# Row sums of squares taken from the transposed copy of x instead of a second load, with a new layout and order in the first phase of a decoder trunk

## The chip, the cores and the metric

The kernel runs on one core of a Trainium2 chip as one program. The metric is the device time of one execution in microseconds; three runs of the kernel before took 1880.76, 1881.30 and 1881.76. The profile comes from one further execution, taken by the hardware profiler.

The engines of a core work through their own queues and meet at semaphores: PE (TensorE) multiplies, ACT (ScalarE) evaluates functions and copies, DVE (VectorE) and POOL (GpSimd) do elementwise work, SP (SyncE) issues the DMA transfers. PEld is PE's loading of weights.

## The reference

The reference is one layer of a hybrid decoder: a mixer of two head groups, a cross-attention into memory tokens, and a gated FFN with a short convolution, for 1024 prompt tokens and 8 x 4 sample tokens (1056 rows of width 1024). The change lies in the beginning of the mixer:

```python
def rms_norm(x, g):
    xf = x.astype(jnp.float32)
    y = xf * lax.rsqrt(jnp.mean(xf * xf, axis=-1, keepdims=True) + EPS)
    return (y * g.astype(jnp.float32)).astype(x.dtype)
...
        u, v, cq, ckv, kpe = split_in(rms_norm(xp, g_mix[l]) @ w_in[l])
        a_out, _ = chunk_gmlp(u, v, w_s[l], b_s[l], ln_v_g[l], ln_v_b[l])
...
def chunk_gmlp(u, v, w_s, b_s, ln_g, ln_b):
    n, t, _ = u.shape
    c = min(t, CHUNK)
    vg = layer_norm(jax.nn.gelu(v).reshape(n, t // c, c, A_GROUPS, A_GROUP_DIM), ln_g, ln_b)
...
    out = jax.nn.gelu(u) * mixed.reshape(n, t, A_WIDTH)
```

## The kernel before

The tokens are numbered 0 to 1055 and cut in two ways: into nine tiles of 128 (`TILES`, the last of 32), and into three chunks of 384, 384 and 288 columns (`CH`). The function `phase1` (from L288) computes the mixer's projections of x. The scale of the norm is not multiplied into x: `rs_tok` (one number per token, tile i in column i) is the `scale` of the Gelu that reads each projection's result (L435 for v, L465 for u), so that products may run ahead of the sums of squares.

**x comes twice.** Transposed, features on the partitions, as `xT` (`xload`, L314 to L317; chunk c, half e of the eight feature blocks, tile `xr`), and once more by tokens, as `x` (`tload`, L319 to L322; 128 tokens of 4 KB each). The transposed copy is scaled by `g_mix` and split into a rounded part and its remainder: `xh` on ACT (L195) and `xl` on DVE (L198, which reads xr and xh). Weights are split in the same way (`wsplit`: `whi` on ACT L191, `wlo` on DVE L192). A projection of one tile (`proj`, L358) is then 24 matmuls: eight feature blocks times `whi·xh`, `wlo·xh`, `whi·xl` (L185). They accumulate in one of five PSUM buffers "mm", which come free when the Gelu of their tile has read them.

**The sums of squares** (`squares`, L324): for each token tile one Square on ACT with an accumulated sum (L332), then eleven small DVE steps for the reciprocal square root (`rsqrt`, L222 to L236). They come in four groups: tile 0; tiles 1 and 2; tiles 3 to 5; tiles 6 to 8.

**Order.** The SP queue is in written order (`manual_schedule`, L336): w_v0 half, chunk 0 half, twice; tile 0 of x; chunk 1; tiles 1 and 2; chunk 2; tiles 3 to 6 of x; w_u0, rows, w_s, w_v1, and tiles 7 and 8. On PE, ACT, DVE and POOL the order is a scheduler's, which places instructions by modelled times. The v projections of the nine tiles are followed by the small matmuls of `gate_matrices` (L394, L396) and the nine u projections; then the same with the second halves of v and u.

After Gelu, v goes in groups of tiles through a layer norm: mean (DVE L436), squares (ACT L440), square root, scaling (DVE L446), then gain and bias on POOL (L448, L450), then a split for the gate (`vgh`, ACT L191).

Of the kernel before, what the change touches and what calls it, by code (L numbers as in the profile page):

```python
# [13 lines left out]
P = 128  # L14
NP_, NS, NT = 1024, 32, 1056
# [5 lines left out]
TILES = [(i * P, P) for i in range(8)] + [(NP_, NS)]  # L21
# [64 lines left out]
def _layout(i):  # L86
# [5 lines left out]
    o["xT"] = f(x.T.reshape(8, P, NT).transpose(1, 0, 2))  # L92

    o["x"], o["mem"] = f(x), f(a["mem_prompt"][0])
    w_in = a["w_in"][0].reshape(8, P, 1568).transpose(1, 0, 2)

    def mtiles(w):
# [57 lines left out]
class Net:  # L155
# [132 lines left out]
    def phase1(self):  # L288
# [5 lines left out]
        pr = self.open("p1r", side="right")  # L294
        raws = {}

        def wraw(name, src, n):
            raws[name] = raw = self.t(pr, [P, 8, 288], F32, "wraw", 2)[:, :, :n]
            for k in range(0, 8, 4):
                nc.sync.dma_start(raw[:, k : k + 4], src[:, k : k + 4])  # L300

        def wsplit(name):
# [5 lines left out]
                self.split(hi[:, k : k + 4], lo[:, k : k + 4], raw[:, k : k + 4])  # L308
            return hi, lo

        px = self.open("px")
        xts, xrs = [], []

        def xload(c, e):  # L314
            o, n = CH[c]
            xrs.append(self.t(px, [P, 4, 384], F32, "xr", 6)[:, :, :n])
            nc.sync.dma_start(xrs[-1], I["xT"][:, 4 * e : 4 * e + 4, o : o + n])  # L317

        def tload(i, place):  # L319
            t0, tn = TILES[i]  # L320
            xts.append(place[:tn])
            nc.sync.dma_start(xts[-1], I["x"][t0 : t0 + tn])  # L322

        def squares(p, i0, i1):  # L324

            ss = self.t(p, [P, 4], F32, "ss", 2)[:, : i1 - i0]
            if i1 == 9:
                nc.vector.memset(ss, 1.0)
            for i in range(i0, i1):
                xt = xts[i]  # L330
                tn = xt.shape[0]
                nc.scalar.activation(xt, xt, AF.Square, accum_out=ss[:tn, i - i0 : i - i0 + 1])  # L332
            self.rsqrt(p, self.rs_tok[:, i0:i1], ss, 1.0 / 1024)

        xt = lambda: self.t(px, [P, 1024], F32, "xt", 3)
        loads = tc.manual_schedule(engines={mybir.EngineType.SP})  # L336
        loads.__enter__()
        raws["v0"] = raw = self.t(pr, [P, 8, 288], F32, "wraw", 2)[:, :, :256]
# [4 lines left out]
        tload(0, xt())  # L343
        for e in range(2):
            xload(1, e)
        tload(1, xt())
        tload(2, xt())
        for e in range(2):
            xload(2, e)
        w = wsplit("v0")  # L350
        for c, (o, n) in enumerate(CH):
            for k in range(8):
                self.split(xh[:, k, o : o + n], xl[:, k, o : o + n], xrs[2 * c + k // 4][:, k % 4], self.col("g_mix", k))
            if c == 0:
                squares(px, 0, 1)
            elif c == 1:
                squares(px, 1, 3)
        def proj(w, i, n):  # L358
            t0, tn = TILES[i]
            ps = self.t(pp, [P, 512], F32, "mm", 5)[:tn, :n]  # L360
# [5 lines left out]
        pl = self.open("pl")  # L366
        a_all = self.t(pl, [P, 9, 512], F32, "a_all")

        flat = a_all.rearrange("p i n -> p (i n)")
        for i in range(3, 7):  # L370
            tload(i, flat[:, (i - 3) * 1024 : (i - 2) * 1024])
        wraw("u0", I["w_u0"], 256)
        pg = self.open("pg")
        rows = self.t(pg, [P, 1024], F32, "rows")
        nc.sync.dma_start(rows, I["rows"][:, :1024].partition_broadcast(P))
        lng, lnb = rows[:, :512], rows[:, 512:]
        gates = {}

        def gate_matrices():

            ws = self.t(pg, [P, 8, P], F32, "ws")
            nc.sync.dma_start(ws, I["w_s"])
            nc.gpsimd.affine_select(ws, ws, [[0, 8], [1, P]], ALU.is_ge, 0.0, base=0, channel_multiplier=-1)
# [3 lines left out]
            sel = self.t(pg, [P, NS], F32, "sel")  # L387
            nc.sync.dma_start(sel, I["c_sel"])
            blk = self.t(pg, [NS, NS], F32, "blk")
            nc.sync.dma_start(blk, I["c_blk"])  # L390
# [3 lines left out]
            nc.tensor.matmul(st[:NS, :32], sel, wsc.rearrange("p g t -> p (g t)"), start=True, stop=True)  # L394
            o_bs, n_bs = COL["bsT"]
            nc.tensor.matmul(st[:NS, 32:40], sel, self.cols[:, o_bs : o_bs + n_bs], start=True, stop=True)  # L396
# [12 lines left out]
        wraw("v1", I["w_v1"], 256)  # L409
        nc.sync.dma_start(self.ident, I["c_ident"])  # L410
        for hf in range(2):
            c0 = hf * 256
            nu = 288 if hf else 256
# [5 lines left out]
            vgs = self.t(pg, [NS, 256], F32, "vgs")  # L419
            for i0, i1 in ((0, 3), (3, 6), (6, 8), (8, 9)):  # L420
                m, tn = i1 - i0, TILES[i0][1]
                if hf == 0 and i0 in (3, 6):
                    squares(pg, i0, i0 + 3)
                if hf == 0 and i0 == 3:
                    for i in range(7, 9):
                        tload(i, flat[:, (i - 7) * 1024 : (i - 6) * 1024])
                    wraw("u1", I["w_u1"], 288)
                    loads.__exit__(None, None, None)
                gv = self.t(pg, [P, 3, 4, 64], F32, "gv", 2)[:tn, :m]
                mu = self.t(pg, [P, 3, 4], F32, "mu", 2)[:tn, :m]  # L430
                rv = self.t(pg, [P, 3, 4], F32, "rv", 2)[:tn, :m]
                for i in range(i0, i1):
                    ps = proj(w, i, 256)
                    g, mi = gv[:, i - i0], mu[:, i - i0]
                    nc.scalar.activation(g.rearrange("p g d -> p (g d)"), ps, AF.Gelu_apprx_tanh, scale=self.rs_tok[:tn, i : i + 1])  # L435
# [19 lines left out]
                if hf == 0 and i0 == 0:  # L455
                    gate_matrices()
                    wsh, wsl, bs_s, wss = (gates[x] for x in ("wsh", "wsl", "bs_s", "wss"))
            if hf == 0:
                w = wsplit("v1")
                wraw("a0", I["w_a"][0], 256)  # L460
            else:
                w = wsplit("a0")
            for i, (t0, tn) in enumerate(TILES):
                ps = proj(wu, i, nu)
# [1084 lines left out]
    def out_proj(self, pp, p, mxs, ws, xh, xl, r3, end):  # L1549
# [4 lines left out]
        def chunk(m, c):  # L1554
            o, n = CH[c]
            wh, wl = ws[m]
            res = self.t(p, [P, 384], F32, "res", 4)[:, :n]
            nc.sync.dma_start(res, I["xT"][:, m, o : o + n])
# [726 lines left out]
```

## Time and profile before

| | value |
|---|---|
| runs, us | 1880.76, 1881.30, 1881.76 (median 1881.3) |
| the profiled execution, its own time, us | 1887.48 |
| its span, first to last instruction, us | 1885.8 |
| mean granted TensorE clock | 0.985 |
| busy PE / DVE / ACT / POOL, us | 1822.9 / 1380.2 / 927.5 / 715.1 |
| DMA over the span | 260.18 MB, mean 138 GB/s |
| DMA from 10 to 20 us | 387 GB/s |

A group row of the profile reads: line, engine, operation, tile written <- tiles read, partitions x elements, count | busy us, mean ns of one | idle time of the engine before them and what ended it. A row in time order begins with its start and its duration. Where several equal instructions follow one another they share a row, and x4 gives their number. Times inside the execution count from the first instruction.

### The profile page before, as it was taken

What the parts mean: (1) busy time and instruction counts of PE and PEld (TensorE: products, weight loads), DVE (VectorE), ACT (ScalarE), POOL (GpSimd) and SP (SyncE); (2) the same over time, 40 slices, a digit from 0 to 9 for tenths busy, and PEclk for the clock granted to TensorE, in tenths of its full rate; (3) what the DMA queues carried; (4) which work ended last, traced back from release to release, by engine and by line L of the source; (5) the groups of instructions that cost most, each with busy time, mean ns of one, the idle gap of its engine ahead of it and who ended that gap; (6) DMA issues with size and microseconds to landing.
All of it is one profiled execution on the core that took longest, in us unless ns stands there. A gap on an engine that the chain in (4) does not pass through costs nothing.

```text
span 1885.8 us, 39848 instructions
## 1 busy us (share of the span) xinstructions
PE 1822.9 (97%) x14402; PEld 1757.2 (93%) x14402; DVE 1380.2 (73%) x2883; ACT 927.5 (49%) x1965; POOL 715.1 (38%) x826
## 2 busy tenths in 40 slices
PE   6999899989999999999999999999999999999999
PEld 6999799889999999998799988999999999999999
DVE  6865967766777667776654676788888888879664
ACT  6435676666555555555443355633332333344442
POOL 1221515643544455444213100157677677500000
PEclk9999899999999999999999999999999999999999
DMA  8102204666765665664564335322222222395252
GB/s 294 60 10 69 80 1 163 228 223 186 213 196 167 187 179 169 175 170 148 171 177 134 134 134 163 128 80 69 91 69 94 77 69 80 99 363 164 79 153 76
DMA packets 135559, 260.18 MB, mean 138 GB/s; under 512 B 20417, under 2 KB 78626, under 8 KB 132290
## 3 DMA queue, kind: packets, MB, share of 16 engines
q1 hardware_dynamic: 134498, 256.58, 43.4%
q8 instruction: 114, 1.87, 0.4%
q10 hardware_dynamic: 864, 1.05, 0.2%
q14 instruction: 83, 0.68, 0.1%
HBM read 212.27 MB, written 45.30 MB: 137 GB/s over the span
## 4 chain that ended last, share of the span: by engine, by line
PE 60%; DVE 6%; issue 4%; DMA 3%; POOL 2%; SPq 1%; ACT 1%; POOLq 0%; DVEq 0%; ACTq 0%
PE d L185 12%; PE s L185 11%; PE b L185 7%; PE F L185 7%; PE X L185 6%; PE E L185 6%; PE A L185 3%; PE y L185 3%; DMA cT<-cT 1%; PE o L1348 1%; DVE mx L1299 1%; POOL S L1296 1%; PE t L185 1%; PE v L185 1%; SPq L1207 1%
## 5 line engine op out<-in xcount | busy, mean ns | idle before, releaser
L185 PE MATMUL s<-w2h,ch 128*128 128x288 f32 (+1 forms) x1024 | 303.8, 297 | 0.0
L185 PE MATMUL s<-w2h,cl 128*128 128x288 f32 (+1 forms) x1024 | 295.1, 288 | 2.7 <-POOL cl L1235 1.4
L185 PE MATMUL s<-w2l,ch 128*128 128x288 f32 (+1 forms) x1024 | 294.7, 288 | 0.0
L185 PEld LDWEIGHTS s<-w2h,ch 128*128 128x128 f32 x1024 | 192.6, 188 | 10.8 <-issue 8.3
L185 PEld LDWEIGHTS s<-w2h,cl 128*128 128x128 f32 x1024 | 192.4, 188 | 3.4 <-POOL cl L1235 1.9
L185 PEld LDWEIGHTS s<-w2l,ch 128*128 128x128 f32 x1024 | 192.8, 188 | 0.0
L1278 DVE TENSOR_REDUCE ss<-sq 128x16 f32<-128x1024 f32 x128 | 155.6, 1215 | 49.3 <-ACT sq L1275 48.4
L1235 POOL TENSOR_TENSOR cl<-cT,ch 128x512 fp32r<-128x512 f32 x64 | 83.7, 1307 | 160.7 <-ACT ch L1231 128.9
L1275 ACT ACTIVATE sq<-s 128x512 f32<-128x512 f32 x128 | 76.5, 598 | 90.0 <-PE s L185 90.0
L1272 ACT ACTIVATE sq<-s 128x512 f32<-128x512 f32 x128 | 76.8, 600 | 78.0 <-PE s L185 78.0
L191 ACT CAST a<-brb 128x528 fp32r<-128x528 f32 x77 | 48.8, 634 | 111.0 <-PE d L185 107.1
L185 PE MATMUL mm<-whi,xh 128*128 128x256 f32 (+3 forms) x288 | 84.5, 294 | 14.4 <-ACT xh L195 9.8
L185 PE MATMUL d<-a,w 128*128 128x264 f32 x768 | 95.4, 284 | 1.0 <-DVE G L2064 1.0
L192 DVE TENSOR_TENSOR a<-brb,a 128x528 fp32r<-128x528 f32 x77 | 54.4, 707 | 57.2 <-ACT a L191 57.1
L185 PEld LDWEIGHTS d<-a,w 128*128 128x128 f32 x768 | 94.3, 188 | 1.1 <-issue 1.1
L185 PE MATMUL mm<-wlo,xh 128*128 128x256 f32 (+3 forms) x288 | 83.3, 292 | 0.0
L185 PE MATMUL mm<-whi,xl 128*128 128x256 f32 (+3 forms) x288 | 83.2, 293 | 0.0
L930 PEld LDWEIGHTS o<-v,pth 128*128 128x128 f32 x576 | 75.9, 197 | 7.3 <-ACT pth L920 5.2
L930 PE MATMUL o<-v,pth 128*128 128x64 f32 x576 | 76.2, 274 | 4.8 <-ACT pth L920 4.4
L1935 POOL TENSOR_TENSOR lo<-s,hi 128x1024 fp32r<-128x1024 f32 x20 | 63.0, 3148 | 45.7 <-ACT hi L1934 45.7
L1231 ACT CAST ch<-cT 128x512 fp32r<-128x512 f32 x128 | 73.5, 627 | 3.9 <-DMA cT<-cT 3.9
L1990 ACT COPY a<-A 128x264 f32<-128x264 f32 x43 | 16.1, 375 | 118.7 <-PE A L185 114.9
(714 smaller groups left out, 6472.2 us busy)
## 6 DMA issues: line engine op xcount, KB each, us to landing
cT<-cT SPq DMA_DIRECT2D x256, 160.0 KB, 2.5
ck<-ck SPq DMA_DIRECT2D x256, 144.0 KB, 3.4
raw<-w_up SPq DMA_DIRECT2D x44, 512.0 KB, 3.6
wsumd<-wsum SPq DMA_DIRECT2D x13, 1024.0 KB, 4.3
actd<-cv SPq DMA_DIRECT2D x44, 264.0 KB, 2.6
brb<-actd SPq DMA_DIRECT2D x44, 264.0 KB, 5.9
wsum<-w_down SPq DMA_DIRECT2D x11, 1024.0 KB, 5.2
raw<-wsumd SPq DMA_DIRECT2D x20, 512.0 KB, 3.8
```

The source lines that it names most:

```text
L185: self.nc.tensor.matmul(out, l, r, start=first and i == 0, stop=last and i == len(seq) - 1)
L191: {"act": nc.scalar.copy, "pool": nc.gpsimd.tensor_copy, "dve": nc.vector.tensor_copy}[eng](hi, src)
L192: low = lambda: nc.vector.tensor_tensor(lo, src, hi, ALU.subtract)
L930: nc.tensor.matmul(u["o"][:, e], th[:, z * P : z * P + P], s["v"][:, jj, h % 4], start=j == z == 0, stop=e == 1 and jj == 2 * G + 1)
L1207: nc.sync.dma_start(ck[j * 32 : j * 32 + 32], I["ck"][bass.ds(rv, 1)].rearrange("a t s f -> (a t) s f"))
L1231: nc.scalar.copy(d["h"][:, k], src[k])
L1235: (nc.vector if k else nc.gpsimd).tensor_tensor(d["l"][:, k], src[k], d["h"][:, k], ALU.subtract)
L1272: nc.scalar.activation(sq[:, 0], ps[:, :, n0 : n0 + 256], AF.Square)
L1275: nc.scalar.activation(sq[:, 1], pt.rearrange("p (e d) -> p e d", e=2), AF.Square)
L1278: yield lambda: nc.vector.tensor_reduce(s["ss"][:, g0 : g0 + 2].rearrange("p e (z h) -> p z e h", z=2), sq.rearrange("p z e (h d) -> p z e ...
L1296: e.tensor_tensor(x, x, ss[:, g0:g1].rearrange("p g h -> p (g h)").unsqueeze(2).broadcast_to([P, n, 4]), ALU.mult)
L1935: eng.tensor_tensor(lo, src, hi, ALU.subtract)
```

## The change

- **Sums of squares.** The input `x`, its nine loads and the Squares by token tile are gone. ACT squares whole halves of the raw transposed chunk (`xr`, four feature blocks x 384 or 288 columns) into free space of `a_all`; POOL adds the two halves, then folds four blocks to two and to one; a matmul with ones over the partitions (`tok_sums`, L270) gives the sums of three tiles in a column each of a PSUM tile `st0`; `rsqrt` runs on three columns at a time, three times.
- **Layout.** `xT` is laid out by chunk, so that one half of a chunk is one run of 6144 B (4608 B) per partition, where it was four of 1536 B (1152 B). The weight tiles `wraw` are packed as well. The later load of `res` reads the same rows from their new place.
- **Warm-up.** `busy` issues four fp32 matmuls on a constant tile and one each on the raw weight half and the raw x half, into `st0`, which is overwritten later.
- **Order.** The v projections of tiles 0 to 5 are issued before the first sums; tiles 5 and 6 use PSUM buffers of the group "st". Tiles 6 and 7 stand behind the Gelu of tiles 0 to 2 in the program, tile 8 and the u projections of tiles 0 and 1 behind that of tiles 3 to 5. `gate_matrices` stands behind all of v. The loads of w_v1, w_s and two small tables move forward in SP's queue.

```diff
-        def squares(p, i0, i1):
-
-            ss = self.t(p, [P, 4], F32, "ss", 2)[:, : i1 - i0]
-            if i1 == 9:
-                nc.vector.memset(ss, 1.0)
-            for i in range(i0, i1):
-                xt = xts[i]
-                tn = xt.shape[0]
-                nc.scalar.activation(xt, xt, AF.Square, accum_out=ss[:tn, i - i0 : i - i0 + 1])
-            self.rsqrt(p, self.rs_tok[:, i0:i1], ss, 1.0 / 1024)
...
+            xrs.append(self.t(px, [P, 4, 384], F32, "xr", 6).rearrange("p k n -> p (k n)")[:, : 4 * n].rearrange("p (k n) -> p k n", k=4))
+            o = 8 * o + 4 * e * n
+            nc.sync.dma_start(xrs[-1].rearrange("p k n -> p (k n)"), I["xT"][:, o : o + 4 * n])
+
+        st0 = self.t(pp, [P, 512], F32, "st", 3)
+        warm = self.t(px, [P, 512], F32, "warm")
+        nc.vector.memset(warm, 1.0)
+
+        def busy(x, n):
+
+            for _ in range(n):
+                nc.tensor.matmul(st0[:, : x.shape[1]], warm[:, :P], x, start=True, stop=True)
+
+        flat = a_all.rearrange("p i n -> p (i n)")
+        places = ((0, 1536), (3072, 1536), (384, 1536))
+
+        def squares(c):
+
+            n = CH[c][1]
+            sq = [flat[:, a : a + 4 * n].rearrange("p (k n) -> p k n", k=4) for a in places[c]]
+            for e in range(2):
+                nc.scalar.activation(sq[e], xrs[2 * c + e], AF.Square)
+            add = lambda a, b: nc.gpsimd.tensor_tensor(a, a, b, ALU.add)
+            a = sq[0]
+            add(a, sq[1])
+            add(a[:, :2], a[:, 2:])
+            add(a[:, 0], a[:, 1])
+            acc = flat[:, places[c][0] : places[c][0] + 384]
+            self.pad(acc, c)
+            return acc
+
+        def roots(c, acc):
+            self.tok_sums(st0, acc, c, self.ones)
+            t = slice(3 * c, 3 * c + 3)
+            self.rsqrt(pl, self.rs_tok[:, t], st0[:, t], 1.0 / 1024)
...
+        busy(warm, 4)
...
+            if e == 0:
+                busy(raw[:, :2].rearrange("p k n -> p (k n)"), 1)
+                busy(xrs[0][:, 0, :256], 1)
...
+            accs.append(squares(c))
...
+        ready = {i: proj(w, i, 256, ("mm", 5) if i < 5 else ("st", 3)) for i in range(6)}
+        roots(0, accs[0])
...
                 if hf == 0 and i0 == 3:
-                    for i in range(7, 9):
-                        tload(i, flat[:, (i - 7) * 1024 : (i - 6) * 1024])
+                    ready[6] = proj(w, 6, 256, ("st", 3))
+                    ready[7] = proj(w, 7, 256)
+                    roots(1, accs[1])
...
+                elif hf == 0 and i0 == 6:
+                    ready[8] = proj(w, 8, 256)
+                    for i in range(2):
+                        us[i] = proj(wu, i, 256)
+                    roots(2, accs[2])
```

Three places show how the instructions stand now. The first is POOL's queue at its start, before: after the memset of `ones` its first work is the gain and bias of v (`gv`, L448, L450).

```order
L258 MEMSET ones_61 128x128
L448 ISA
L448 TENSOR_TENSOR gv_232<-gv_232,rows_217 128x256 x3
L450 TENSOR_TENSOR gv_232<-gv_232,rows_217 128x256 x3
L383 AFFINE_SELECT ws_361<-ws_361 128x1024
L392 COPY wsc_372<-ws_361 128x32
```

POOL's queue at the same place now: nine adds of squares (L343) stand ahead of v's gain and bias (now L469, L471), with the affine select of the gate matrix (`ws`) ahead of the last.

```order
L258 MEMSET ones_61 128x128
L343 ISA
L343 TENSOR_TENSOR a_all_90<-a_all_90 128x1536
L343 TENSOR_TENSOR a_all_90<-a_all_90 128x768
L343 TENSOR_TENSOR a_all_90<-a_all_90 128x384
L343 TENSOR_TENSOR a_all_90<-a_all_90 128x1536
L343 TENSOR_TENSOR a_all_90<-a_all_90 128x768
L343 TENSOR_TENSOR a_all_90<-a_all_90 128x1152
L343 TENSOR_TENSOR a_all_90<-a_all_90 128x384
L343 TENSOR_TENSOR a_all_90<-a_all_90 128x576
L402 AFFINE_SELECT ws_202<-ws_202 128x1024
L343 TENSOR_TENSOR a_all_90<-a_all_90 128x288
```

The adds of chunks 1 and 2 are interleaved; v's gain and bias come only when all are through.

The second place is DVE's queue now, from chunk 1's remainders on (`xr_112` and `xr_114` are its halves, `xr_116` and `xr_118` those of chunk 2, `wlo_378` belongs to w_u0, `st_94` holds the sums of squares).

```order
L198 SCALAR_TENSOR_TENSOR xl_83<-xr_112,cols_58,xh_82 128x384 x4
L198 SCALAR_TENSOR_TENSOR xl_83<-xr_114,cols_58,xh_82 128x384 x4
L198 SCALAR_TENSOR_TENSOR xl_83<-xr_116,cols_58,xh_82 128x288 x4
L198 SCALAR_TENSOR_TENSOR xl_83<-xr_118,cols_58,xh_82 128x288 x4
L192 TENSOR_TENSOR wlo_378<-wraw_191,whi_377 128x4x256
L222 TENSOR_SCALAR rqx_40_362<-st_94 128x3
L192 TENSOR_TENSOR wlo_378<-wraw_191,whi_377 128x4x256
L223 TENSOR_SCALAR rqy_42_364<-rqx_40_362 128x3
L224 TENSOR_SCALAR rqy_42_364<-rqy_42_364 128x3
```

Where before the square roots of tiles 0 to 2 stood among these remainders, all sixteen now come first, then the split of w_u0, then the root of tiles 0 to 2.

The third is ACT's queue now, with the Squares (L342) among the roundings of x (L195); `whi_377` belongs to w_u0.

```order
L195 ACTIVATE xh_82<-xr_110,cols_58 128x384 x4
L342 ACTIVATE a_all_90<-xr_110 128x1536
L195 ACTIVATE xh_82<-xr_112,cols_58 128x384 x4
L342 ACTIVATE a_all_90<-xr_112 128x1536
L195 ACTIVATE xh_82<-xr_114,cols_58 128x384 x4
L195 ACTIVATE xh_82<-xr_116,cols_58 128x288 x4
L195 ACTIVATE xh_82<-xr_118,cols_58 128x288 x2
L342 ACTIVATE a_all_90<-xr_114 128x1536
L195 ACTIVATE xh_82<-xr_118,cols_58 128x288 x2
L191 CAST whi_377<-wraw_191 128x4x256 x2
L342 ACTIVATE a_all_90<-xr_116 128x1152
L342 ACTIVATE a_all_90<-xr_118 128x1152
```

The Square of chunk 1's second half stands ahead of the last two roundings of chunk 2, and it writes where the first POOL add reads, so it comes after that add. The Gelu of tiles 0 to 2 stand behind these rows.

More of the change, by code (lines that the diff above doesn't have):

```diff
@@ L91, in _layout @@
     o = {}
[L92 to L94 removed]
+    xT = x.T.reshape(8, P, NT).transpose(1, 0, 2)
+    o["xT"] = f(np.concatenate([xT[:, :, c : c + n].reshape(P, 8 * n) for c, n in CH], 1))
+    o["mem"] = f(a["mem_prompt"][0])
     w_in = a["w_in"][0].reshape(8, P, 1568).transpose(1, 0, 2)
@@ L295, in phase1, with wtile @@
         raws = {}
+        def wtile(n):
+            return self.t(pr, [P, 8, 288], F32, "wraw", 2).rearrange("p k n -> p (k n)")[:, : 8 * n].rearrange("p (k n) -> p k n", k=8)
         def wraw(name, src, n):
-            raws[name] = raw = self.t(pr, [P, 8, 288], F32, "wraw", 2)[:, :, :n]
+            raws[name] = raw = wtile(n)
             for k in range(0, 8, 4):
@@ L309, in wsplit @@
             return hi, lo
+        pl = self.open("pl")
+        a_all = self.t(pl, [P, 9, 512], F32, "a_all")
         px = self.open("px")
-        xts, xrs = [], []
+        xrs = []
         def xload(c, e):
             o, n = CH[c]
[L316 to L322, printed above, removed]
@@ L342, in phase1 @@
             xload(0, e)
[L343 to L349, printed above, removed]
+            if e == 0:
+                busy(raw[:, :2].rearrange("p k n -> p (k n)"), 1)
+                busy(xrs[0][:, 0, :256], 1)
+        for c in (1, 2):
+            for e in range(2):
+                xload(c, e)
         w = wsplit("v0")
+        accs = []
         for c, (o, n) in enumerate(CH):
@@ L365, in phase1 @@
         self.close("px")
[L366 to L371, printed above, removed]
         wraw("u0", I["w_u0"], 256)
+        wraw("v1", I["w_v1"], 256)
         pg = self.open("pg")
@@ L376, in phase1 @@
         lng, lnb = rows[:, :512], rows[:, 512:]
+        ws = self.t(pg, [P, 8, P], F32, "ws")
+        nc.sync.dma_start(ws, I["w_s"])
+        sel = self.t(pg, [P, NS], F32, "sel")
+        nc.sync.dma_start(sel, I["c_sel"])
+        blk = self.t(pg, [NS, NS], F32, "blk")
+        nc.sync.dma_start(blk, I["c_blk"])
         gates = {}
         def gate_matrices():
-            ws = self.t(pg, [P, 8, P], F32, "ws")
-            nc.sync.dma_start(ws, I["w_s"])
             nc.gpsimd.affine_select(ws, ws, [[0, 8], [1, P]], ALU.is_ge, 0.0, base=0, channel_multiplier=-1)
@@ L454, in phase1 @@
                         nc.sync.dma_start(O["o_vg"][:, c0 : c0 + 256], vgs)
-                if hf == 0 and i0 == 0:
-                    gate_matrices()
-                    wsh, wsl, bs_s, wss = (gates[x] for x in ("wsh", "wsl", "bs_s", "wss"))
             if hf == 0:
+                gate_matrices()
+                wsh, wsl, bs_s, wss = (gates[x] for x in ("wsh", "wsl", "bs_s", "wss"))
                 w = wsplit("v1")
```

25 lines of the change are left out of this document (7 added, 18 removed).

## The prediction

> **What bounds the kernel now.** I read the page first, then the busy times by stretch of phase 1, then the instructions of each engine in time order.
>
> ```profile
> span 1885.8 us, 39848 instructions
> PE 1822.9 (97%) x14402; PEld 1757.2 (93%) x14402; DVE 1380.2 (73%) x2883; ACT 927.5 (49%) x1965; POOL 715.1 (38%) x826
> ```
>
> PE is busy in 97% of the span, so only what moves PE counts. The stretches (columns: busy time and instructions of PE, PEld, DVE, ACT, POOL, then granted PE clock, DMA share, GB/s) show where PE loses time early:
>
> ```profile
> 9.80:15.20 5.40, 5.40 (x25) 5.40 (x26) 5.15 (x9) 4.96 (x9) 0.00 (x0) 1.00 1.06 382
> 15.20:35.20 20.00, 20.00 (x169) 19.80 (x167) 15.31 (x61) 15.93 (x35) 0.00 (x0) 1.00 0.71 256
> 35.20:39.83 4.63, 0.00 (x0) 0.00 (x1) 4.49 (x20) 3.76 (x6) 0.00 (x0) 0.91 1.06 373
> 39.83:45.80 5.97, 5.97 (x28) 4.97 (x29) 5.82 (x13) 2.46 (x6) 5.96 (x7) 0.50 1.08 359
> 46.00:170.00 124.00, 124.00 (x917) 120.98 (x916) 82.50 (x262) 50.62 (x109) 29.21 (x35) 1.00 0.14 43
> ...
> PE mm L185 <- ACT gv L435: 4.6, 1, 4.6
> ```
>
> PE starts slowly (5.40/25 = 0.216 us a matmul), multiplies without a break from 15.2 to 35.2 (20.00/169 = 0.118), stands still for 4.63 us, then runs 28 matmuls at clock 0.50 (5.97/28 = 0.213 each, 28 x 0.095 = 2.7 us lost). After 46 it is busy 124.00 of 124.00 us. So whatever shifts phase 1 is carried on to the end, and this can be measured at one place: the first matmul of u tile 2, the first piece of PE work that stands behind the same set of matmuls in both kernels. Before, it follows the gate's two small matmuls:
>
> ```profile
> 51.02 0.25 PE L394 MATMUL st<-wsc,sel 128*32 128x32 f32 x2
> 51.11 0.21 PE L396 MATMUL st<-cols,sel 128*32 128x8 f32 x2
> 51.24 0.38 PE L185 MATMUL mm<-whi,xl 128*128 128x256 f32 x1
> ```
>
> The place is 51.3. The 4.63 us stall waits for a PSUM buffer, and that for the Gelu of tile 3, whose scale comes from squares of x that land late (ACT in time order):
>
> ```profile
> 9.13 2.13 ACT L195 ACTIVATE xh<-xr,cols 128x384 fp32r<-128x384 f32 x4 [1.72 <-DMA xr<-xT]
> 11.17 1.03 ACT L191 CAST whi<-wraw 128x1024 fp32r<-128x1024 f32 x1
> 12.64 2.13 ACT L195 ACTIVATE xh<-xr,cols 128x384 fp32r<-128x384 f32 x4 [0.44 <-DMA xr<-xT]
> 14.68 1.04 ACT L332 ACTIVATE xt<-xt 128x1024 f32<-128x1024 f32 x1
> ...
> 30.85 1.06 ACT L332 ACTIVATE a_all<-a_all 128x1024 f32<-128x1024 f32 x1 [1.29 <-DMA a_all<-x]
> ...
> 39.30 0.84 ACT L435 ACTIVATE gv<-mm,rs_tok 128x256 f32<-128x256 f32 x2 [0.18 <-DVE rs_tok L236]
> ```
>
> The change removes that load and so attacks a real stall: 4.63 + 2.7 = 7.3 us stand there, and 25 x 0.098 = 2.4 more at the start.
>
> **What it puts in its place.** Six Squares of whole raw halves on ACT, then nine adds on POOL (1536, 768, 384 columns for chunks 0 and 1; 1152, 576, 288 for chunk 2), all between 17 and 42, when DVE makes the xl halves of the split. Until now POOL did nothing there:
>
> ```profile
> 39.84 2.51 POOL L448 TENSOR_TENSOR gv<-gv,rows 128x256 f32<-128x256 f32 x3 [38.82 <-ACT gv L435]
> ```
>
> So this overlap is new, and I looked for other places where POOL adds while DVE reads two tiles from SBUF, as xl does (xr and xh). First the DVE, then the POOL rows:
>
> ```profile
> 64.88 0.70 DVE L224 TENSOR_SCALAR rqy<-rqy 32x4 int32<-32x4 int32 x1
> ...
> 67.01 0.67 DVE L235 SCALAR_TENSOR_TENSOR rqh<-rqa 32x4 f32<-32x4 f32 x1
> 67.71 0.15 DVE L236 SCALAR_TENSOR_TENSOR rqy<-rqh,rqy 32x4 f32<-32x4 f32 x1
> ...
> 64.77 1.49 POOL L448 TENSOR_TENSOR gv<-gv,rows 128x256 f32<-128x256 f32 x2 [6.14 <-DVE gv L446]
> 66.22 1.44 POOL L450 TENSOR_TENSOR gv<-gv,rows 128x256 f32<-128x256 f32 x2
> ```
>
> The DVE operations from 64.88 to 67.01, four of four columns each, take 0.66 to 0.70, one for each POOL operation, and 0.15 as soon as POOL is through. Each waits out one POOL operation, and POOL takes its turn after each. The same at full size:
>
> ```profile
> 1309.54 1.16 DVE L1958 TENSOR_TENSOR l<-raw,h 128x512 fp32r<-128x512 f32 x1
> 1310.63 3.52 DVE L2032 TENSOR_TENSOR G<-G,row 128x1056 f32<-128x1056 f32 x1
> ...
> 1281.55 1.26 DVE L2069 TENSOR_TENSOR cv<-cv,G 128x1056 f32<-128x1056 f32 x1
> ...
> 1310.12 2.91 POOL L2053 TENSOR_TENSOR cv<-cv,row 128x1056 f32<-128x1056 f32 x1
> 1312.98 2.33 POOL L1952 TENSOR_TENSOR s<-raw,raw 128x512 f32<-128x512 f32 x1
> ...
> L2040 DVE SCALAR_TENSOR_TENSOR cv<-G,cols,cv x44: 726/764/1772, 1221.9 to 1641.2; 128x528 f32<-128x528 f32 x22, 128x496 f32<-128x496 f32 x22
> ```
>
> L2032 needs 1.26 alone (L2069, same shape) and took 3.52: it ended at 1314.15, 1.12 after POOL's L2053 at 1313.03. L1952 waited for it in turn. L2040, an operation of xl's own kind, shows the wait as well (median 0.764, longest 1.772). [...]
>
> **The sum, step by step.** Prices first (group rows: count, busy time and mean in ns; then rows of DVE in time order):
>
> ```profile
> L1337 POOL TENSOR_TENSOR S<-S,bc 128x1056 f32<-128x1056 f32 x7 | 17.3, 2474 | 7.6 <-ACT bc L1336 7.6
> L1296 POOL TENSOR_TENSOR S<-S,ss 128x768 f32<-128x768 f32 x8 | 16.1, 2013 | 47.5 <-DVE ss L236 47.5
> L1383 POOL TENSOR_TENSOR raw<-raw,cols 128x1024 f32<-128x1024 f32 x4 | 7.6, 1898 | 6.8 <-DVE xl L192 3.2 <-DMA raw<-w_mq 3.1 <-DMA res<-res 0.5
> L1935 POOL TENSOR_TENSOR lo<-s,hi 128x1024 fp32r<-128x1024 f32 x20 | 63.0, 3148 | 45.7 <-ACT hi L1934 45.7
> L383 POOL TENSOR_SCALAR_AFFINE_SELECT ws<-ws 128x1024 f32<-128x1024 f32 x1 | 1.3, 1287 | 0.0
> ...
> 12.23 1.23 DVE L192 TENSOR_TENSOR wlo<-wraw,whi 128x1024 fp32r<-128x1024 f32 x1 [0.25 <-ACT whi L191]
> 13.38 2.20 DVE L198 SCALAR_TENSOR_TENSOR xl<-xr,cols,xh 128x384 fp32r<-128x384 f32 x4
> 16.04 0.15 DVE L223 TENSOR_SCALAR rqy<-rqx 128x1 int32<-128x1 int32 x1
> 16.22 0.15 DVE L224 TENSOR_SCALAR rqy<-rqy 128x1 int32<-128x1 int32 x1
> ...
> L198 DVE SCALAR_TENSOR_TENSOR xl<-xr,cols,xh 128x288 fp32r<-128x288 f32 x8 | 3.9, 515 | 0.0
> ```
>
> 1. *When POOL begins.* A Square of 1536 columns is not in the trace; 1.04 for 1024 gives at most 1.56 and, with a fixed part, about 1.45. xh of the first half ends at 11.26; Square to 12.7; the cast to 13.7; the second xh (2.13, pitch about 2.05) to 15.75; Square to 17.2.
>
> 2. *Adds.* L1337 is 2.474/1056 = 2.34 ns a column: 3.6 for 1536, 2.7 for 1152, 1.35 for 576, 0.9 for 384 (I take 1.0), 0.7 for 288 (0.8); L1296 gives 2.0 for 768. Chunks 0 and 1: 6.6 each; chunk 2: 4.85; the scheduler puts the affine select (1.3) ahead of the last add. Sum 19.35. Bounds: by L1383 (1.85 ns) 18.05 x 1.85/2.34 + 1.3 = 15.6; by L1935 (3.07 ns, which has waits in it) 25.0.
>
> 3. *xl.* Behind 17.2 stand eight of 384 at 2.20/4 = 0.55 and eight of 288 at 0.515: 8.5. One that has waited is about 0.14 shorter (1.12 against 1.26, and L2053's 1313.03 - 1310.70 = 2.33 against 2.47); for 19 hand-overs that is -2.7.
>
> 4. *The last xl.* If the two take turns, nothing overlaps: 17.2 + 19.35 + 8.5 - 2.7 = 42.4. Where POOL waits for a Square (about 24.5 to 26.5) DVE runs several xl on end, which the sum has already. Without any waits ACT's last xh, near 27, would set it, the last xl near 27.7. The loss is 14.7 us on DVE. Part of it PE hides: tile 3 waits for chunk 1's first xl, and tile 6 takes its eight steps one by one as the xl of chunk 2 come, so it ends at 42.6 instead of about 30.4.
>
> 5. *rs_tok.* In DVE's queue behind the last xl stand two wlo of u (1.23 each, the first step of the square root between them) and ten more steps, 0.18 apart for one column and taken as 0.2 for three: 2.45 + 2.0 = 4.5, so 46.9. Gelu of tile 0 (0.84/2 = 0.42) ends at 47.3. Tile 7 needs its PSUM buffer: PE stalls from 42.6 to 47.4, 4.8 us, as long as the stall that was removed.
>
> 6. *PE from there to u tile 2*: tiles 7, 8, u0, u1, 96 matmuls. A stall of 4.63 was followed by 28 matmuls at 0.213, so I take that again: 6.0 + 68 x 0.118 = 14.0; the two sums by ones (18 small matmuls and their waits, an estimate from the gate's small ones above, 0.1 apiece less overlap) 1.1; gate 0.3. 47.4 + 15.4 = 62.8. The Gelu of tile 3, whose buffer u tile 2 takes, comes at about the same time, behind casts that wait for six POOL operations of 0.84 to 0.91 (2.51 and 2.73 for three, L448, L450).
>
> 62.8 - 51.3 = **+11.5 us**. The other parts: four constant and two raw multiplications on PE before 9 lie in its idle time, and where they raise PE's speed at the start (2.4 us above), tiles 0 to 2 still wait for xh and xl and end before the first held xl, so they gain nothing here. Longer runs: DMA ran at 387 GB/s between 10 and 20 already (x rows of 4 KB and xT rows of 1.5 KB mixed), 0; the loads of v1, ws, sel and blk land earlier than they are needed, 0. The 4.3 MB of x fall out of a DMA that no longer decides, 0.
>
> [...]
>
> The profiled execution took 1887.48 (span 1885.8 and 1.7 around it), the median of the three runs 1881.3. Profiled I expect 1887.5 + 11.5 = 1899.0, timed 1881.3 + 11.5 = **1892.8**.
>
> **Rivals.**
>
> *No waits between POOL and DVE (faster).* [...] For it: ACT and PE are left alone by POOL, and L198 itself has never been seen beside POOL. Against it: every row above. It decides if xl stays near 0.55 after 17.2.
>
> *POOL starves instead (no change).* If DVE's queue, which is full, keeps the memory until its xl are through, the adds begin near 27.7; chunk 0's end at 34.3, and Sq1b, which needs a buffer of the first add, comes at 31.3, with the last two xh behind it. [...] Against it: L1952 got its turn after one DVE operation, and so did each L448.
>
> *Longer adds and a lower clock during the dribble of tile 6 (slower still).* By L1935's price +5.65, 17.2 in all: 1898.5. Against it: its rows include waits. By L1383's price -3.75: +7.7, 1889.0; with the clock kept after the stall another -2.7, 1886.3.
>
> **Chances.** Turns, at any of these prices: 0.77. No waits: 0.14. POOL starves, or losses and gains balance: 0.09. Differences under 0.2% (3.8 us) can hardly be told from no change; the cases fall on its three sides: slower 0.77, same 0.09, faster 0.14. The likeliest case alone spans 1886.3 to 1898.5; the range, 1882 to 1900, also takes in gains that offset part of the wait, and leaves the faster case out.
>
> **What would show it.** Right: POOL's L343 of 1536 columns at 17.2, 3 to 4 us long; beside it an xl of about 3.5, then xl of 1.3 to 3 one after each add; the last xl between 38 and 47; PE idle for 4 to 5 us ahead of tile 7; u tile 2 near 63, and PE without gaps behind it. Wrong: xl at 0.5 to 0.6 throughout (the first rival), POOL waiting until 27 (the second), or a later phase with idle PE time in which the shift is lost; before 170 there is none, and behind it I have only the 97%.

## The result, and the profile after

| | before | changed |
|---|---|---|
| runs, us, median | 1881.73 (6 runs, 1880.76 to 1884.43) | 1893.87 (6 runs, 1893.13 to 1896.65) |
| ratio, 95% interval | | 1.0065, 1.0054 to 1.0076 |
| profiled execution / its span | 1887.48 / 1885.8 | 1894.05 / 1892.2 |
| u tile 2 begins in the profile | 51.6 | 60.4 |

The change is 12.1 us slower; 1892.8 was forecast. The prediction takes 51.3 for the start of u tile 2 before, from the row at 51.24. By count that row is the last matmul of u tile 1: it is number 264, the end of the eleventh projection of 24, and a `whi,xl`, the kind with which every projection ends. The first of u tile 2 stands behind it, here before and then changed:

```profile
51.56 0.38 PE L185 MATMUL mm<-whi,xh 128*128 128x256 f32 x1
...
60.44 0.39 PE L185 MATMUL mm<-whi,xh 128*128 128x256 f32 x1 [0.77 <-ACT gv L456]
```

Some of POOL's and DVE's rows in time order (start, duration) show the chunk sums beside the split of x. First POOL, then DVE, of the changed kernel:

```profile
15.99 3.49 POOL L343 TENSOR_TENSOR a_all<-a_all 128x1536 f32<-128x1536 f32 x1 [14.98 <-ACT a_all L342]
19.56 2.02 POOL L343 TENSOR_TENSOR a_all<-a_all 128x768 f32<-128x768 f32 x1
25.35 3.94 POOL L343 TENSOR_TENSOR a_all<-a_all 128x1536 f32<-128x1536 f32 x1 [2.49 <-ACT a_all L342]
31.28 2.86 POOL L343 TENSOR_TENSOR a_all<-a_all 128x1152 f32<-128x1152 f32 x1
...
16.45 3.45 DVE L198 SCALAR_TENSOR_TENSOR xl<-xr,cols,xh 128x384 fp32r<-128x384 f32 x1 [0.58 <-ACT xh L195]
19.82 2.17 DVE L198 SCALAR_TENSOR_TENSOR xl<-xr,cols,xh 128x384 fp32r<-128x384 f32 x1
23.20 0.61 DVE L198 SCALAR_TENSOR_TENSOR xl<-xr,cols,xh 128x384 fp32r<-128x384 f32 x1
31.55 2.90 DVE L198 SCALAR_TENSOR_TENSOR xl<-xr,cols,xh 128x288 fp32r<-128x288 f32 x1
38.41 1.05 DVE L198 SCALAR_TENSOR_TENSOR xl<-xr,cols,xh 128x288 fp32r<-128x288 f32 x1
```

The xl issued at 16.45 ends at 19.90, 0.42 behind POOL's end at 19.48: it waited for the add, or was held by it, as it is called below. POOL waits in its turn: the add of 1536 columns at 25.35, issued while an xl ran, took 3.94, the one at 15.99, when none ran, 3.49. The third DVE row falls where POOL waits for a Square, and is back at 0.61. The same from a distance, the group rows of the stretch from 15 to 41:

```profile
L198 DVE SCALAR_TENSOR_TENSOR xl<-xr,cols,xh 128x288 fp32r<-128x288 f32 x8 | 14.0, 1822 | 0.0
L198 DVE SCALAR_TENSOR_TENSOR xl<-xr,cols,xh 128x384 fp32r<-128x384 f32 x10 | 10.6, 1126 | 0.6 <-ACT xh L195 0.6
```

Chunk 2's xl takes 1822 ns where it took 515. The last of them ends at 39.88. PE's waits (us in total, times, longest) and stretches (columns as in the prediction):

```profile
PE mm L185 <- ACT gv L456: 4.7, 2, 4.0
PE mm L185 <- DVE xl L198: 3.0, 2, 1.6
PE st L185 <- DVE xl L198: 2.2, 3, 1.0
...
20.00:30.00 10.00, 8.53 (x46) 8.18 (x47) 10.00 (x9) 9.76 (x16) 7.36 (x4) 0.66 0.51 204
40.70:44.67 3.97, 0.03 (x1) 0.00 (x0) 3.06 (x13) 0.50 (x2) 0.00 (x0) 0.50 0.40 108
44.67:50.50 5.83, 5.81 (x35) 5.74 (x35) 5.40 (x21) 2.87 (x6) 0.00 (x0) 0.66 0.37 148
62.00:180.00 118.00, 118.00 (x868) 115.40 (x867) 79.53 (x255) 46.77 (x103) 29.62 (x34) 1.00 0.10 30
```

The stall of 4.63 at 35 is gone; one of 3.97 at 40.7, again followed by a half-speed stretch, and 5.2 us of waits for xl stand in its place. The clock was also down between 20 and 30 (0.66), which the prediction's sum does not have; it moves nothing here, since PE still waits 2.2 us for xl in tile 6 behind it. Behind 62 PE has no gap to 180.

### The profile page after: what moved, and what is told of

Its sections match the earlier page's. It is cut to its first block, busy times and chain, and to the rows that moved or that the text cites. A ratio compares the mean times of both kernels' runs of the same rounds, so it can differ in the third digit from the quotient of the medians.

```text
span 1892.2 us, 39881 instructions
## 1 busy us (share of the span) xinstructions
PE 1832.5 (97%) x14432; PEld 1762.9 (93%) x14432; DVE 1394.1 (74%) x2872; ACT 924.0 (49%) x1953; POOL 738.8 (39%) x836
## 3 DMA queue, kind: packets, MB, share of 16 engines
q1 hardware_dynamic: 127154, 252.25, 42.7%
## 4 chain that ended last, share of the span: by engine, by line
PE 61%; DVE 5%; issue 4%; DMA 3%; POOL 2%; SPq 2%; ACT 1%; POOLq 0%; DVEq 0%; ACTq 0%
PE d L185 12%; PE s L185 12%; PE b L185 7%; PE F L185 7%; PE X L185 7%; PE E L185 7%; PE A L185 3%; PE y L185 3%; PE o L1368 1%; DMA cT<-cT 1%; DVE mx L1319 1%; POOL S L1316 1%; DMA raw<-mix 1%; SPq L1223 1%; SPq L1227 1%
## 5 line engine op out<-in xcount | busy, mean ns | idle before, releaser
L185 PEld LDWEIGHTS s<-w2h,ch 128*128 128x128 f32 x1024 | 193.0, 189 | 10.8 <-issue 8.3
L185 PE MATMUL mm<-whi,xh 128*128 128x256 f32 (+3 forms) x272 | 79.7, 295 | 4.7 <-ACT gv L456 4.7
L185 PE MATMUL mm<-whi,xl 128*128 128x256 f32 (+3 forms) x272 | 78.8, 294 | 3.0 <-DVE xl L198 3.0
L185 PE MATMUL mm<-wlo,xh 128*128 128x256 f32 (+3 forms) x272 | 78.1, 290 | 0.0
```

What stands on the lines that cost most here:

```text
L185: self.nc.tensor.matmul(out, l, r, start=first and i == 0, stop=last and i == len(seq) - 1)
```

## The experiments

All of them in one table first. "At 100 us" is the median, over the PE, ACT and DVE instructions of 100 to 180 us that both traces have equally often, of their start less their start in the second profile of before (below); by this the first profile of before stands at +0.9. The time is less the median of the runs of before taken with it.

| kernel | u tile 2 | at 100 us | timed against before, us | ratio, 95% interval |
|---|---|---|---|---|
| the change | 60.4 | +9.8 | +12.1 | 1.0054 to 1.0076 |
| adds_dve | 53.2 | +4.1 | +4.1 | 1.0007 to 1.0039 |
| pool_writes | 50.8 | +2.9 | +4.8 | 1.0010 to 1.0030 |
| no_busy | 60.8 | +10.0 | +9.3 | 1.0036 to 1.0064 |
| old_layout | 61.1 | +10.8 | +11.3 | 1.0035 to 1.0063 |
| early_space | 45.4 | -2.0 | -0.2 | 0.9987 to 1.0017 |
| kept_load | 41.4 | -7.5 | -9.1 | 0.9935 to 0.9963 |
| kept_load_cold | 42.7 | -7.4 | -6.5 | 0.9958 to 0.9982 |
| mended | 52.2 | +1.8 | +3.6 | 1.0006 to 1.0031 |
| adds_twice | 77.1 | +40.7 | +41 (one run) | |

**adds_dve.** Is xl long because of POOL's adds (the turns of the prediction), or because the Squares come late?

```diff
-            add = lambda a, b: nc.gpsimd.tensor_tensor(a, a, b, ALU.add)
+            add = lambda a, b: nc.vector.tensor_tensor(a, a, b, ALU.add)
```

> The nine adds of the squares run on DVE instead of POOL; nothing else is edited (the scheduler then spreads them among the xl operations of chunks 1 and 2). Theory (a POOL add and an xl exclude each other, so POOL's 21 us of adds and gate work are added to DVE's time): the adds cost DVE about 1.04 ns a column, 7392 columns or 7.7 us instead, no xl is longer than 0.65, the last xl ends near 29 to 31 (changed kernel: 39.8), and u tile 2 starts at 48 to 50.5 instead of 60.4: about 10 us faster than the changed kernel, 1882 to 1885. Rival (the late sums come from ACT's Squares and the order, and xl is only long because it waits for something else): DVE's queue grows by 7.7 us while nothing leaves it, so u tile 2 comes later than 60.4 and the time is 1895 to 1902.

Measured: 1886.21 (11 runs), 7.7 less than the change. Some of DVE's rows:

```profile
17.50 1.76 DVE L343 TENSOR_TENSOR a_all<-a_all 128x1536 f32<-128x1536 f32 x1
19.18 1.67 DVE L198 SCALAR_TENSOR_TENSOR xl<-xr,cols,xh 128x384 fp32r<-128x384 f32 x3
25.61 1.75 DVE L343 TENSOR_TENSOR a_all<-a_all 128x1536 f32<-128x1536 f32 x1
27.28 3.07 DVE L198 SCALAR_TENSOR_TENSOR xl<-xr,cols,xh 128x288 fp32r<-128x288 f32 x5
31.14 0.50 DVE L198 SCALAR_TENSOR_TENSOR xl<-xr,cols,xh 128x288 fp32r<-128x288 f32 x1
```

More work on DVE ends its xl sooner, at 31.6 instead of 39.9: the rival falls. The one xl above 0.65 (1.35) is among the five at 27.28; it stands beside the affine select, which was left on POOL. The gain is smaller than expected (53.2, not 48 to 50.5): this execution's first xh came at 9.59, 1.6 later than the change's, and the scheduler put the small adds and two square roots between each other, so that rs_tok of tiles 0 to 2 is ready only at 38.8. Before tile 7 PE waits 4.2 us for sums.

**pool_writes.** Is it POOL's being busy, or its reading? The sums of squares become constants here, so rs_tok, and what hangs on it, is not computed.

```diff
-            add = lambda a, b: nc.gpsimd.tensor_tensor(a, a, b, ALU.add)
+            add = lambda a, b: [nc.gpsimd.memset(a, 0.125) for _ in range(3)]
```

> Each add on POOL is replaced by three memsets of the same target, so POOL is busy for about as long (0.9 ns a column and memset, 1.4 us three times for 1536) but reads nothing; the sums of squares are then constants, so that part of the result is left out. Theory (what excludes xl is POOL's reading of SBUF): xl stays at 0.5 to 0.65 beside a busy POOL, the last xl ends at 26 to 28, u tile 2 starts at 45 to 48, 1879 to 1883. Rival (any long POOL instruction holds DVE up, or the waits come from semaphores between POOL and the others, which all stay): xl of 1.5 to 4 us beside the memsets, last xl near 38 to 42, 1892 to 1896.

Measured: 1886.99 (12 runs). POOL's memsets, and some of DVE's rows beside them:

```profile
13.66 18.51 POOL L343 MEMSET a_all<- 128x1536 f32 x22
...
17.06 2.21 DVE L198 SCALAR_TENSOR_TENSOR xl<-xr,cols,xh 128x384 fp32r<-128x384 f32 x4 [0.59 <-ACT xh L195]
20.46 2.21 DVE L198 SCALAR_TENSOR_TENSOR xl<-xr,cols,xh 128x384 fp32r<-128x384 f32 x4 [1.19 <-ACT xh L195]
26.55 1.81 DVE L198 SCALAR_TENSOR_TENSOR xl<-xr,cols,xh 128x288 fp32r<-128x288 f32 x4 [0.96 <-ACT xh L195]
28.27 0.16 DVE L222 TENSOR_SCALAR rqx<-st 128x3 f32<-128x3 f32 x1
28.47 3.09 DVE L223 TENSOR_SCALAR rqy<-rqx 128x3 int32<-128x3 int32 x1
28.77 2.78 DVE L192 TENSOR_TENSOR wlo<-wraw,whi 128x1024 fp32r<-128x1024 f32 x1
31.59 0.60 DVE L224 TENSOR_SCALAR rqy<-rqy 128x3 int32<-128x3 int32 x1
```

POOL is busy from 12 to 34, and no xl is longer than 0.62 (four in 2.21): the memsets, which only write, did not hold it. The last xl ends at 28.4, close to the 26 to 28 of the theory. The place of u tile 2 (50.8, not 45 to 48) and the time miss: the Gelu of tile 0 comes at 35.5, since a step of the square root (L223, 0.15 alone) took 3.09 beside the memsets, and wlo behind it 2.78; a later step waited 0.9 for the affine select. The 3.09 was not foreseen; it is taken up at the end.

**adds_twice.** The change with each add followed by one of the same size.

```diff
-            add = lambda a, b: nc.gpsimd.tensor_tensor(a, a, b, ALU.add)
+            add = lambda a, b: [nc.gpsimd.tensor_tensor(a, a, b, ALU.add), nc.gpsimd.tensor_tensor(b, b, a, ALU.add)]
```

> The changed kernel with a second POOL add behind each add of squares, of the same size, into a place that nothing reads any more; the scheduler puts one add of 768 and one of 1152 between others and some of the smallest behind the xl. Theory (one POOL operation for one xl, turn by turn, none overlapping): no xl longer than 4 us (one POOL add and itself), two of nearly 4 in a row where there was one, the last xl at 50 to 55 instead of 39.9, that is later by the time of the POOL operations that were added ahead of it and by nothing else; u tile 2 15 to 20 us later. Rival 1 (POOL's whole backlog goes first): an xl of 7 us or more. [...]

Measured: 1925.54 (one run). POOL, then DVE:

```profile
16.93 3.49 POOL L343 TENSOR_TENSOR a_all<-a_all 128x1536 f32<-128x1536 f32 x1 [15.91 <-ACT a_all L342]
20.50 3.63 POOL L343 TENSOR_TENSOR a_all<-a_all 128x1536 f32<-128x1536 f32 x1
...
17.39 3.45 DVE L198 SCALAR_TENSOR_TENSOR xl<-xr,cols,xh 128x384 fp32r<-128x384 f32 x1 [0.59 <-ACT xh L195]
20.76 3.80 DVE L198 SCALAR_TENSOR_TENSOR xl<-xr,cols,xh 128x384 fp32r<-128x384 f32 x1
```

Two long adds, and between them exactly one xl: strict turns, neither a backlog of POOL's nor a preference for DVE. The last xl ends at 51.7, 11.8 later than in the change, and u tile 2 comes 16.7 later. Against the change, 30.9 us stand at 100 us. Only the 11.8 are the split's; the rest are longer waits further on, among them 5.4 us for the Gelu of tile 3 at 71.7, behind steps of a square root of 0.64 to 1.32 each beside POOL's late adds, and 7.9 us at 100.9 for POOL's part of the last layer norm, which was not followed up.

**no_busy** and **old_layout** take back one side part each.

```diff
-        busy(warm, 4)
...
-            if e == 0:
-                busy(raw[:, :2].rearrange("p k n -> p (k n)"), 1)
-                busy(xrs[0][:, 0, :256], 1)
```

> The changed kernel without the six warm-up multiplications. Theory (as in the prediction: tiles 0 to 2 end before the first held xl with or without them, so they are worth nothing while POOL holds xl): PE runs at 0.213 a matmul from about 8.5 to 14, the start of tile 3 does not move, u tile 2 within 0.3 of 60.4, same time (1893 to 1895). Rival (the lost 2.4 us at the cold start are carried on): u tile 2 at 62.5 to 63, 2 to 2.6 us slower than the changed kernel.

Measured: 1891.48 (5 runs). Between 9 and 15 us PE runs 32 matmuls, against 50 in the change, and u tile 2 is at 60.8 against 60.4, the time not longer (at 2.4 less, within what such runs scatter). The warm-up does what it says and is worth nothing here, since tiles 0 to 2 end before the first held xl either way (at 18.2 against 19.9 in the change, at 20.0 against 20.3 here).

```diff
-    o["xT"] = f(np.concatenate([xT[:, :, c : c + n].reshape(P, 8 * n) for c, n in CH], 1))
+    o["xT"] = f(xT)
...
-            nc.sync.dma_start(xrs[-1].rearrange("p k n -> p (k n)"), I["xT"][:, o : o + 4 * n])
+            nc.sync.dma_start(xrs[-1], I["xT"][:, 4 * e : 4 * e + 4, o : o + n])
```

> The changed kernel with the transposed x in its former layout (runs of 1536 B), all else as changed. In the changed kernel the first xh began at 8.03, before at 9.13. Theory A (the longer runs bring the first halves sooner): first xh 0.4 to 1.1 later, and with it every xl and u tile 2 by about as much (61 to 61.5), 0.5 to 1 us slower. Theory B (as the prediction has it, run length is worth nothing; the profiled start of the two executions differed by itself): first xh and u tile 2 within 0.3 of the changed kernel's, same time.

Measured: 1893.42 (5 runs), no different from the change. From the first weight cast to the first xh, that is from the landing of the first weight half to that of the first half of x, pass

```profile
5.87 1.04 ACT L191 CAST whi<-wraw 128x1024 fp32r<-128x1024 f32 x1 [3.57 <-DMA wraw<-w_v]
8.03 1.12 ACT L195 ACTIVATE xh<-xr,cols 128x384 fp32r<-128x384 f32 x2 [1.11 <-DMA xr<-xT]
```

2.16 us in the change, and in old_layout

```profile
6.01 1.05 ACT L191 CAST whi<-wraw 128x1024 fp32r<-128x1024 f32 x1 [3.71 <-DMA wraw<-w_v]
8.72 0.62 ACT L195 ACTIVATE xh<-xr,cols 128x384 fp32r<-128x384 f32 x1 [1.67 <-DMA xr<-xT]
```

2.71. Other profiles have 1.93 to 2.48 with the new layout and 2.20 to 2.77 with the old, so longer runs may bring the first half some 0.4 us sooner; as the ranges overlap, this is not settled, and no time shows it.

**before_again.** Why do the profiled spans differ by 6.4 where the times differ by 12?

> The kernel before, profiled a second time. At 100 us the profiled change stands 8.8 us behind the first profile of before, at the end only 6.6, while the timed medians are 12 apart; the clock records show half speed in multiples of 3.41 us at places that differ between executions. Theory (the first profile of before was one of its long executions, by half-speed stretches behind 200 us that fall by chance): phase 1 repeats within 1 us, the stall of 4.6 at 35 too, the half-speed time behind 100 us differs by one or more multiples of 3.41, and the span is 2 to 6 us shorter than 1885.8. Rival (the change gains 2 us in later phases): the second profile has the first one's times behind 200 us within 1 us.

Measured: span 1878.8, 7.0 less than the first profile; 1880.5 timed. Phase 1 repeats: the stall at 34.6 is 4.83, u tile 2 starts at 50.3, and at 100 us the two are 0.9 apart. The other 6.1 us come behind 200. One of those places in both (before, then before again; clock in the third column from the right):

```profile
212.00:242.00 30.00, 25.13 (x136) 21.88 (x135) 25.46 (x99) 18.86 (x55) 5.47 (x10) 0.72 0.14 56
...
212.00:242.00 30.00, 24.05 (x158) 21.24 (x157) 25.47 (x100) 20.00 (x52) 4.49 (x8) 0.89 0.10 39
```

PE is busy about equally long and gets through 136 and 158 matmuls. The first profile of before was a long one, and the comparison of spans with it says 5 to 6 us too little. This kernel stands ahead of the change by 13.4 us of span.

**early_space** and **kept_load** ask whether the stall could be removed without POOL.

```diff
+        pl = self.open("pl")
+        a_all = self.t(pl, [P, 9, 512], F32, "a_all")
         px = self.open("px")
...
-        xt = lambda: self.t(px, [P, 1024], F32, "xt", 3)
+        xt = lambda: self.t(px, [P, 1024], F32, "xt", 2)
```

> The kernel before, with the tile a_all opened ahead of the pool of raw x (two buffers for the first token tiles instead of three pay for it), so that the loads of token tiles 3 to 6 need not wait until raw x is free; nothing else. Theory (the stall of 4.6 us at 35 comes from those late loads, and needs no new way of summing): their Squares run at 27 to 32 instead of 31 to 36, tile 3's Gelu comes near 35 instead of 39.3, the stall at 35 shrinks below 1 us; a later wait, for buffers of the u tiles, takes part of it back, so 1 to 4 us faster than before. Rival (the Squares wait for ACT and DMA, not for space): Squares and stall as before, same time.

Measured: 1883.07 (12 runs) beside 1883.31. In the trace the theory holds: the Squares of tiles 3 to 6 begin at 26.86 (before 30.85), the Gelu of tile 3 at 34.10 (before 39.30), and the stall at 35 is gone; 1.3 us at 54.8 are the longest wait. But five waits of 0.3 to 1.3, 3.7 us in all, come between 39 and 69, for POOL, ACT and DVE. At 100 us 2.0 are left of the 4.6, and in the time nothing that can be told.

kept_load adds other parts of the change, without its sums and its layout, and one that the change does not have: four v projections of the second half (`early`) stand ahead of the gate's matmuls.

```diff
+        busy(warm, 8)
...
+                busy(raw[:, 0], 2)
+                busy(xrs[0][:, 0, :256], 1)
...
-                    ps = proj(w, i, 256)
+                    ps = early.pop(i) if i in early else proj(w, i, 256, ("st", 3) if hf == 0 and i in (5, 6) else ("mm", 5))
...
-                if hf == 0 and i0 == 0:
-                    gate_matrices()
...
+                gate_matrices()
...
+            if hf == 0:
+                early = {i: proj(w, i, 256) for i in range(4)}
```

> The second load of x and the Squares by token tile as before, with early_space's earlier space, the change's warm-up, tiles 5 and 6 in other PSUM buffers, the gate's matrices behind v, and the first four v projections of the second half ahead of the gate's matmuls. POOL adds nothing in phase 1. Theory (the change's order is worth several us once no POOL add stands beside xl): no PE gap over 1 us before 100 us but near 8, u tile 2 near 41 to 44 (before 51.3), what stands at 100 us in before comes 7 to 10 us earlier, time 1872 to 1876. Rival (DVE's chain of layer norms bounds phase 1 anyway): PE waits ahead of the gate's matmuls for as long as it gained, time within 3 us of before.

Measured: 1874.22 (6 runs) beside 1883.31, ratio 0.9949, its whole interval below 1. PE from 9 on (two rows of windows, one of waits):

```profile
9.00:15.00 6.00, 5.99 (x50) 5.86 (x50) 5.62 (x10) 5.80 (x12) 0.00 (x0) 1.00 1.06 405
15.00:100.00 85.00, 83.61 (x687) 81.26 (x687) 74.98 (x243) 45.57 (x95) 27.85 (x30) 1.00 0.41 144
...
PE mm L185 <- ACT gv L448: 1.3, 2, 0.9
```

1.4 us idle in 85, clock 1.00. The second load of x is still there, so that load as such need not cost time. Its wait for space is only a part of what did: removed alone, in early_space, it brought 2.0 of the 7.5 us at 100. The other parts were not tried one by one, but for the warm-up (below). This is the version that beats both kernels. Its profiled execution is the longest of the six (1883.37), so its span says nothing.

> kept_load without the warm-up multiplications. Theory (where xl is not held, the cold start is carried to the end): PE at 0.213 a matmul from about 9 to 15, u tile 2 and all behind it 2 to 3 us later than in kept_load. Rival (tiles 0 to 2 wait for xh and xl in any case, as they did in the change): within 0.5 us of kept_load.

Measured: 1876.86 (12 runs). The warm-up's 50 against 34 matmuls between 9 and 15 are 1.4 us at u tile 2, and nothing at 100 us (-7.4 and -7.5): kept_load's 1.3 us of waits stand around the gate's matmuls, at 74.9 and 77.3, and kept_load_cold, which comes later, has none there. The timed 2.6 us between them has overlapping intervals and no place in the trace up to 100; it stays open.

**mended.** The change's own way, with adds_dve's edit and kept_load's four early projections.

```diff
+            if hf == 0:
+                early = {i: proj(w, i, 256) for i in range(4)}
```

> The change with its adds on DVE (as adds_dve) and four v projections of the second half ahead of the gate's matmuls, as in kept_load. Theory (with the adds on DVE the wait for rs_tok ahead of tile 7 stays at 6 to 7.5 us, and the wait ahead of the gate's matmuls goes away): what stands at 100 us 5 to 7 us ahead of adds_dve's place for the v projections behind the gate, time 1879 to 1884, about that of before. Rival (DVE's work, longer by 7.7 us of adds, bounds the phase): same as adds_dve, 1885 to 1888.

Measured: 1888.02 (12 runs) beside 1884.43. The early projections come 5.7 us sooner than in adds_dve (the first at 72.1 against 77.8), but that is their new place in the order and no gain. The wait at the gate that they were to fill was only 1.0 us long in adds_dve; it is gone, and PE has no gap from 39 to 130:

```profile
38.93:83.50 44.57, 44.57 (x360) 44.14 (x361) 39.84 (x128) 20.12 (x44) 16.47 (x18) 0.95 0.15 49
83.50:130.00 46.50, 46.50 (x359) 44.83 (x358) 31.80 (x103) 13.33 (x30) 15.72 (x18) 1.00 0.03 5
```

The lead over adds_dve is 2.3 us at 100, 1.0 of it there at u tile 2 already, and none in the time (+3.6 and +4.1). The time is near the rival's, but its reason is not shown: PE no longer waits behind 39, while the 4.2 us for sums ahead of tile 7 remain. With the sums on DVE this phase is no faster than before.

## Why the prediction was right, point by point

- **POOL and DVE take turns.** Shown by the rows of the change, by adds_twice (one xl between two long adds), by adds_dve (xl short without POOL's adds: 0.65 at most but for one of 1.35 beside the affine select), and by pool_writes (0.62 at most beside memsets, which read nothing, so POOL's being busy alone did not hold xl). This was the step with the sign in it. One of its four small rows, L224 at 64.88, is no example of two tiles read: it reads one (see the last section).
- **When POOL begins:** 17.2 forecast, 15.99 measured. The Square of 1536 was 1.48 (1.45 taken); the first xh came 1.1 earlier than in the profile of before.
- **Sum of the adds:** 19.35 forecast with the affine select; measured 20.6 with the waits inside the records: 7.4 and 4.0 for the pairs of 1536 and 768, 2.9, 2.4, 1.6, 1.0 and 1.3. Without the waits it is 17.4, each add counted from the end of the xl before it. So L1337's rate fits the records, while the sum without waits lies halfway between its 19.35 and the 15.6 by L1383's; by L1935's it would have been 25.
- **The last xl:** 42.4 forecast, 39.88 measured. From POOL's start that is 25.2 against 23.9. The adds without waits were 2.0 less than taken (17.4 for 19.35), and the sixteen xl as well (6.5 for 8.5, as an xl that waited ends 0.3 to 0.4 behind the add, and the next one otherwise 0.43 or 0.53 behind the last); 2.7 had been taken off for the hand-overs, 4.0 were saved.
- **rs_tok and the stall:** 4.5 from the last xl to rs_tok, measured 4.2 (44.07). The stall, forecast 4.8, is 3.97, and the clock did fall: 0.66 over the 5.8 us behind it.
- **PE to u tile 2:** 15.4 forecast, 15.8 measured (44.67 to 60.44). So u tile 2 is 8.9 late, not 11.5: 0.3 by the place taken for before (51.3 for 51.6), 1.2 by the earlier start, 1.3 by the hand-overs, while the two steps above differ by 0.4 at most and nearly cancel.
- **Carried to the end, one for one.** This step was too simple. In the table, place at 100 us and timed difference agree to within 2.4 us and lie on both sides of each other, so no cover behind 100 takes the shift away; but the change shows +9.8 in the one and +12.1 in the other. The forecast of 1892.8 is so near 1893.87 by luck: a shift that was forecast 1.7 to 2.6 too large (11.5, where 9.8 stand at 100 us and 8.9 at u tile 2) met something of about that size behind 100 which the sum did not have. What it is for the timed runs cannot be seen, since only profiled executions have a trace. In the profiles the half-speed stretches of the last section are a part of it, not always the whole: kept_load's loses 10.4 us behind 100 on the second profile of before, with 13.7 us more of half speed, which are worth 6.8 at most.
- **What was costed at nothing** (warm-up, layout) moved no measured time in no_busy and old_layout. The missing 4.3 MB were not tried alone.
- **The rivals.** No waits: refuted, no xl stayed short that was issued while a POOL add ran. That POOL leaves ACT alone fits before's trace: the 66 casts of 1024 columns there (L1934) take 1.045 to 1.060, beside POOL's work or not. POOL starves: refuted for xl by adds_twice.

## What to carry to other kernels

Before work moves to an idle POOL, look what DVE does at that time: here xl, with two inputs in SBUF, and POOL's adds, which read there, took turns (xl of 288 columns 1.82 us beside the adds, 0.515 before), so POOL's time (2.3 ns a column) was added to DVE's instead of hidden. A stall that ends on a late load should first be asked why the load was issued late: here opening one tile earlier removed it, where the new way of summing made another. And a gain in one phase is worth what is left at its end: in early_space more than half of the wait removed at 35 came back as smaller waits behind it, and in kept_load the warm-up's 1.4 us ended as a wait at the gate.

## What was not expected of the hardware

**A POOL instruction that only writes held another kind of DVE instruction.** In pool_writes xl and the second wlo (31.67 to 32.90), with two inputs from SBUF, ran at their own length beside memsets. A TENSOR_SCALAR on three columns that reads and writes SBUF (L223) took 3.09 instead of 0.15, and here there were no turns: five memsets ended while it waited. L224, of the same form, took 0.60 and 0.35 in its two places. All three end in a gap between two POOL instructions (31.53 to 31.59, 32.17 to 32.23, 34.00 to 34.03); while L223 waited ahead of the first of these gaps, each memset's record began some 0.05 before the last one's end. L222, which reads PSUM, took 0.16. Three rows in one profile show this; what sets L223 and L224 apart from xl was not shown.

**Half-speed stretches came in multiples of 3.413 us.** The trace's clock records of the two profiles of before (start on the trace's own scale and length in us; those at 0.5 behind 115 us, without the last one, which the end of the execution breaks off):

```
before        227.56 17.07   323.13 6.83   432.36 6.83   947.77 6.83   971.66 3.41   1050.17 6.83
before again  231.65  6.83   320.40 6.83   426.21 6.83   945.04 6.83                 1044.02 6.83
```

Every length is a multiple of 3.413 us. The twelve profiles have 9 to 14 times that length in this part of the program, mostly at the same few places, where PE has waited one to four us (in the first profile of before 1.06 to 4.43 us; other waits there of 1.20 to 1.66 us have no half speed behind them); the sum is 34.1 us in the second profile of before and 47.8 in the first. By an estimate from these sums the difference of 13.7 is worth 6.8 us at most, at half speed, and 6.1 us is by how much the two move apart behind 100. Why the lengths are such multiples, and why two executions of one program have different ones, was not shown. For a change of 10 us it means: compare medians of runs, and places in the trace ahead of such stretches, never two spans.
